# A two-layer hybrid encoder on one core: split value slabs two halves ahead, and gate and modulation slabs in half steps

## The chip, the core and the metric

The kernel runs on one core of one Trainium2 chip. The metric is the device time of one execution in microseconds (us); three runs of the kernel before gave 2033.23, 2034.02 and 2035.17 us, so the median is 2034.02 us. The engines spoken of are PE (TensorE, matrix multiply), DVE (VectorE), ACT (ScalarE) and SP (SyncE, which here issues nearly all DMAs). POOL (GpSimd) does no work of note.

## What is computed

One sequence of 256 tokens, width 1024, goes through two layers. Layer 0 mixes tokens with a gated linear recurrence (HGRN2), layer 1 with an RG-LRU block; each is followed by a PEER feed-forward part, and every sub-layer has an RMSNorm with shift, scale and gate that come from a conditioning vector (`mod = silu(c) @ w_ada + b_ada`, a 1024 x 6144 matrix for each layer). The change touches the PEER part alone:

```
def peer_ffn(h, w_q, sub_keys, u_tab, v_tab):      # 16384 experts, 8 heads, 16 experts each
    ...                                            # ids, gate: top-16 experts per token and head
    u = u_tab[idx]
    act = gelu(einsum('thkd,td->thk', u, hx))
    return einsum('thk,thkd->td', gate * act, v_tab[idx])
```

The kernel does not gather experts. It multiplies all tokens with all of `u_tab` (stage u), applies gelu, multiplies the result by a dense table of gates that is zero for experts not chosen, and multiplies that with all of `v_tab` (stage v). All weights are read from HBM once, in slabs of 128 x 2048 float32 (1 MB).

## The kernel before, in words

**Stages.** For each layer: mixer, then `peer(i)`: queries and routing, stage u (64 slabs of `u_tab`, `s1`), stage v (64 slabs of `v_tab`, `s2`). The change acts in stage v, which runs from about 711 to 1073 us in layer 0 and from 1665 to 2019 us in layer 1 of the profiled execution.

**Stage v.** A slab g holds values of 256 experts and is worked off in two halves of 128 experts. A float32 operand is split into a high and a low part of type float32r (`split`, lines 297 to 302: ACT copies the high part, DVE subtracts it to get the low part). For each half, `prep` (line 1280) splits the slab's half into a buffer of `WS` (tile `wsplit`, a ring of 3) and the gated activations of these experts into a slot of `box_wt` (tile `gsplit`, a ring of 4; lines 1288 and 1289); `mm` (line 1291) is 12 matmuls of 512 columns on line 1297: four with both high parts, four with the low part of the activations (they wait for line 1289), four with the low part of the slab. `push` (line 285) calls `prep` at once and puts `mm` into a list; as soon as the list holds more than `depth` (1) entries the oldest is emitted. So in the program the preparation of a half stands one half ahead of its matmuls. On the chip the engines run freely, and how far ACT and DVE get ahead of PE is set by the rings.

**Slabs and slots.** One list, `order`, says in which order slabs of all kinds are fetched, and `pump` (line 197) issues the next of them on SP's queue as soon as a slot of the list `allowed` is free. `take` picks the next slab of the list up, `free` returns its slot and calls `pump`. At the start of stage v only three slots (14, 15 and 16) are in `allowed`, since all others hold activations; slots 0 to 2 join after slab 17 (`release(0, 1, 2)` at line 1333, whose activations have been used), and in layer 0 five more after slab 33. A slot is free when the DVE subtraction of the slab's second half has ended.

**Other slabs in stage v.** Sixteen slabs "gd" for each layer hold the dense gates. Two of them cover the activations of eight slabs of values, so a pair stands in the list ahead of slab max(0, 8q - `GLEAD`), with `GLEAD` = 2: ahead of 0, 6, 14, 22 and so on. `gates()` (line 1238) multiplies the activations by one of them in one DVE instruction of 2048 elements per partition (line 1244); both of a pair run one after the other. In layer 0, 24 slabs "ada" (weights of the modulation) stand behind slabs 13, 15, 17 and so on; `ada_slab` (line 388) takes one in two DVE instructions of 1024 elements (line 394), one after the other. At slab 4 the residual (`XT`, 1 MB, line 1331) is read back through the same SP queue.

**Side work.** `side` emits pieces of other work after a group of matmuls: in layer 0 at the start of stage v, `load_cond` (eight small DVE, line 374, and PE, line 375, pairs and an ACT copy, line 382) and `softplus` (small DVE instructions and one ACT table load); in layer 1 after slab 44, `pre_final` (16 transposes on PE, line 1373, with ACT copies, and eight of the pairs of lines 374 and 375).

Of the kernel before, what the change touches and what calls it, by code (L numbers as in the profile page):

```python
# [16 lines left out]
AF = mybir.ActivationFunctionType  # L17
OP = mybir.AluOpType
AX = mybir.AxisListType

P = 128
# [19 lines left out]
ADA_OPEN = 4  # L41
ADA_T0 = 13
ADA_TE = 2
GLEAD = 2
GS16 = 32768.0
C_ROUTE = 1.9
C_G0 = 2.15
# [25 lines left out]
def body(ctx, tc, A, out):  # L73
# [34 lines left out]
    def slabs(v, n):  # L108
        a = at(v)
        assert a + n <= (NSL if v < NSL else NSL + NRAW)  # L110
        return AR[:, a:a + n]

    def slab(v):
        return AR[:, at(v)]
# [100 lines left out]
    def take(kind):  # L215
        n = st["taken"]
        assert order[n][0] == kind, (order[n], kind)
        assert n < st["issued"], (n, order[n])
        st["taken"] += 1
        return n, AR[:, at(held[n])]  # L220

    def free(n):
        del held[n]
        pump()
# [6 lines left out]
    def release(*slabs):  # L231
        for z in slabs:
            assert z not in allowed
            allowed.append(z)
        pump()
# [56 lines left out]
    def flush():  # L292
        while queue:
            run_one()
        run_posts(0)

    def split(raw):
        n = wsn[0] % NWS
        wsn[0] += 1
        ACT.activation(WS[:, n, 0], raw, AF.Copy)  # L300
        V.tensor_tensor(WS[:, n, 1], raw, WS[:, n, 0], op=OP.subtract)  # L301
        return WS[:, n, 0], WS[:, n, 1]

    def mm3(o, ws, rs, ks, start=True, stop=True):
        wh, wl = ws
# [79 lines left out]
        yield from row_bcast(cs, bank)  # L385
        cond_copy(bank)

    def ada_slab():
        n, raw = take("ada")
        i, s = order[n][1:]  # L390
        for m in range(2):
            col = 2 * s + m
            r_ = raw[:, m * 1024:(m + 1) * 1024]
            V.scalar_tensor_tensor(r_, r_, 1.0, cb, op0=OP.mult, op1=OP.mult, accum_out=mod[:, i, col:col + 1])  # L394
        free(n)
        if s % 4 == 3:
            c0 = 2 * (s - 3)
            V.tensor_tensor(mod[:, i, c0:c0 + 8], mod[:, i, c0:c0 + 8],
                            sv("b_ada")[:, i * 48 + c0:i * 48 + c0 + 8], op=OP.add)
            if c0 == 40:  # L400

                V.tensor_scalar(mod[:, i, c0:c0 + 8], mod[:, i, c0:c0 + 8], 1.0 / GS16, None, op0=OP.mult)

    def weaved():
        while st["taken"] < len(order) and order[st["taken"]][0] == "ada":
            ada_slab()

    epst = pool.tile([P, 2], F32, name="eps")
    V.memset(epst, EPS)
# [604 lines left out]
    def peer(i):  # L1014
# [149 lines left out]
        def aslab(j):  # L1164
            s = j // 8
            return s if s < NSL else s + 3
# [71 lines left out]
        def gates():  # L1238

            n, raw = take("gd")  # L1240
            q, th = order[n][2] // 2, order[n][2] % 2
            av = slabs(aslab(16 * q), 2).rearrange("p a (j t) -> p (a j) t", t=S)[:, :, th * P:(th + 1) * P].rearrange(
                "p j (g t) -> p j g t", t=8)
            V.tensor_tensor(av, av, raw.rearrange("p (g j t) -> p j g t", g=16, t=8), op=OP.mult)  # L1244
            free(n)

        box_wt = []
        wtn = [0]
# [1 line left out]
        def s2(cost):  # L1250
            n, raw = take("v")
            g = order[n][2]
            if g == 63 and i == 1:
                boxes = []

                def prep():
                    for half in range(2):
                        hi, lo = split(raw[:, half * 1024:(half + 1) * 1024])
                        w_ = box_wt[0][:, (wtn[0] + half) % 4]
                        ACT.activation(w_[:, 0], acol(126 + half), AF.Copy)  # L1260
                        V.tensor_tensor(w_[:, 1], acol(126 + half), w_[:, 0], op=OP.subtract)
                        boxes.append((w_, (hi, lo)))
                    free(n)

                def mm():
                    for tb in range(2):
                        for dh in range(2):
                            for z, (w_, r_) in enumerate(boxes):
                                for a, v_ in ((0, 0), (1, 0), (0, 1)):
                                    PE.matmul(PS[:, 4 + 2 * tb + dh], w_[:, a, tb * P:(tb + 1) * P],  # L1270
                                              r_[v_][:, dh * 512:(dh + 1) * 512], start=False,
                                              stop=(z, a, v_) == (1, 0, 1), skip_group_check=True)

                push(prep, mm, None, cost)
                return
            for half in range(2):
                j = 2 * g + half
                box = {}

                def prep(half=half, j=j, box=box):  # L1280
                    hi, lo = split(raw[:, half * 1024:(half + 1) * 1024])
                    if half == 1:
                        free(n)
                    z = wtn[0] % 4
                    wtn[0] += 1
                    box["v"] = (hi, lo)
                    box["z"] = z
                    ACT.activation(box_wt[0][:, z, 0], acol(j), AF.Copy)  # L1288
                    V.tensor_tensor(box_wt[0][:, z, 1], acol(j), box_wt[0][:, z, 0], op=OP.subtract)  # L1289

                def mm(j=j, box=box):
                    hi, lo = box["v"]
                    z = box["z"]
                    sets = ((0, hi), (1, hi), (0, lo))
                    steps = [(a, r, tb, dh) for a, r in sets for tb in range(2) for dh in range(2)]
                    for a, r, tb, dh in steps:
                                PE.matmul(PS[:, 4 + 2 * tb + dh], box_wt[0][:, z, a, tb * P:(tb + 1) * P],  # L1297
                                          r[:, dh * 512:(dh + 1) * 512], start=(j == 0 and a == 0 and r is hi),
                                          stop=False, skip_group_check=True)

                push(prep, mm, None, cost)
# [16 lines left out]
        if i == 0:  # L1318
            sides.append(cond)
            sides.append(softplus())  # L1320
        for it in vs[i]:
            if it[0] == "ada":
                settle(cond)
                weaved()
                continue
            if it[0] == "gd":
                gates()
                continue
            g = it[2]
            if g == 4:  # L1330
                nc.sync.dma_start(XT, Xd[i])
            elif g == 18:
                release(0, 1, 2)
            elif g == 34 and i == 0:
                release(3, 4, 5, 6, 7)
            elif g == 52 and i == 0:
                reserve(0, 1, 2, 3, 4, 5, 6)
            elif g == 58 and i == 0:
                release(13)
            s2(C_G1)  # L1340
            if g == 63 and i == 1:
                flush()
            if i == 1 and g == 44:
                sides.append(pre_final())
        if i == 0:
            release(17, 18)

# [154 lines left out]
```

## Time and profile before

| | us |
|---|---|
| median of three runs | 2034.02 |
| profiled execution, time | 2034.58 |
| profiled execution, span of the core | 2032.8 |
| stage v of layer 0, first to last matmul of line 1297 | 710.66 to 1073.05 |
| stage v of layer 1, the same | 1665.46 to 2018.81 |
| busy in the span: PE / DVE / ACT | 1952.5 / 1588.4 / 1002.4 |

PE is busy for 96% of the span, so a microsecond is won or lost where PE waits. A matmul's recorded duration overlaps its neighbours' (389 ns recorded at a distance of about 227 ns), so waits are read from start times and counts rather than from durations.

### The profile page before, as it was taken

What the parts mean: (1) busy time and instruction counts of PE and PEld (TensorE: products, weight loads), DVE (VectorE), ACT (ScalarE), POOL (GpSimd) and SP (SyncE); (2) the same over time, 40 slices, a digit from 0 to 9 for tenths busy, and PEclk for the clock granted to TensorE, in tenths of its full rate; (3) what the DMA queues carried; (4) which work ended last, traced back from release to release, by engine and by line L of the source; (5) the groups of instructions that cost most, each with busy time, mean ns of one, the idle gap of its engine ahead of it and who ended that gap; (6) DMA issues with size and microseconds to landing.
All of it is one profiled execution on the core that took longest, in us unless ns stands there. A gap on an engine that the chain in (4) does not pass through costs nothing. (4 is left out here: it accounts for less than half of the span.)

```text
span 2032.8 us, 32119 instructions
## 1 busy us (share of the span) xinstructions
PE 1952.5 (96%) x12862; PEld 1783.3 (88%) x12862; DVE 1588.4 (78%) x2791; ACT 1002.4 (49%) x1419; POOL 0.2 (0%) x4
## 2 busy tenths in 40 slices
PE   7999999999999999999999989999999999999998
PEld 6898899999999977888888889999999998888786
DVE  6798659997898777888877776998889966676575
ACT  3544544444555454444445744444545554544454
POOL 0000000000000000000000000000000000000000
PEclk9999999999999999999999999999999999999999
DMA  8654713446666767989753472444666777766561
GB/s 351 270 193 165 285 69 133 172 173 207 226 210 222 256 248 259 400 342 406 290 207 149 162 302 92 164 169 177 207 224 207 235 260 261 295 248 260 206 232 58
DMA packets 125765, 456.87 MB, mean 225 GB/s; under 512 B 7720, under 2 KB 73512, under 8 KB 74672
## 3 DMA queue, kind: packets, MB, share of 16 engines
q1 hardware_dynamic: 59056, 421.27, 55.7%
q10 hardware_dynamic: 66560, 33.56, 5.6%
q8 instruction: 100, 1.64, 0.3%
q14 instruction: 49, 0.40, 0.1%
HBM read 418.10 MB, written 36.70 MB: 224 GB/s over the span
## 5 line engine op out<-in xcount | busy, mean ns | idle before, releaser
L301 DVE TENSOR_TENSOR wsplit<-arena,wsplit 128x1024 fp32r<-128x1024 f32 x600 | 729.1, 1220 | 328.6 <-ACT wsplit L300 327.3
L300 ACT ACTIVATE wsplit<-arena 128x1024 fp32r<-128x1024 f32 x600 | 630.8, 1057 | 543.1 <-PE psum L1297 307.0
L1297 PE MATMUL psum<-wsplit,gsplit 128*128 128x512 f32 x3048 | 700.2, 391 | 8.8 <-DVE gsplit L1289 5.0
L1297 PEld LDWEIGHTS psum<-wsplit,gsplit 128*128 128x128 f32 x3048 | 572.5, 188 | 133.8 <-DVE gsplit L1289 11.0
L308 PE MATMUL psum<-hsplit,wsplit 128*128 128x256 f32 x2448 | 610.3, 287 | 1.0 <-ACT wsplit L300 0.8
L309 PE MATMUL psum<-hsplit,wsplit 128*128 128x256 f32 x2448 | 601.5, 283 | 0.0
L308 PEld LDWEIGHTS psum<-hsplit,wsplit 128*128 128x128 f32 x2448 | 470.2, 192 | 3.7 <-ACT wsplit L300 1.9
L309 PEld LDWEIGHTS psum<-hsplit,wsplit 128*128 128x128 f32 x2448 | 471.0, 192 | 0.1
L311 PE MATMUL psum<-hsplit,wsplit 128*128 128x256 f32 x2448 | 347.7, 285 | 16.8 <-DVE wsplit L301 16.7
L311 PEld LDWEIGHTS psum<-hsplit,wsplit 128*128 128x128 f32 x2448 | 316.2, 192 | 23.3 <-DVE wsplit L301 22.9
L1182 ACT ACTIVATE arena<-psum 128x512 f32<-128x512 f32 x128 | 76.1, 594 | 247.7 <-PE psum L311 247.7
L1289 DVE TENSOR_TENSOR gsplit<-arena,gsplit 128x256 fp32r<-128x256 f32 x254 | 106.1, 418 | 0.0
L1215 DVE TENSOR_TENSOR xT<-psum,xT 128x512 f32<-128x512 f32 x128 | 84.4, 684 | 22.6 <-ACT xT L1214 22.0
L1288 ACT ACTIVATE gsplit<-arena 128x256 fp32r<-128x256 f32 x254 | 101.5, 399 | 0.0
L394 DVE SCALAR_TENSOR_TENSOR arena<-arena,scratch 128x1024 f32<-128x1024 f32 x80 | 94.1, 1220 | 0.0
L1198 DVE TENSOR_TENSOR gsplit<-scratch 128x2048 f16<-128x2048 f16 x64 | 77.9, 1217 | 0.0
L1207 PE MATMUL psum<-gsplit,scratch 128*128 128x256 f16 x512 | 70.4, 274 | 5.6 <-DVE xT L1215 3.9
L1214 ACT ACTIVATE xT<-psum 128x512 f32<-128x512 f32 x128 | 71.9, 594 | 5.3 <-PE psum L1207 4.6
L1244 DVE TENSOR_TENSOR arena<-arena 128x2048 f32<-128x2048 f32 x32 | 71.9, 2284 | 0.1
L1207 PEld LDWEIGHTS <-scratch 128*128 128x128 f16 x512 | 43.8, 98 | 14.0 <-issue 6.6
L697 DVE TENSOR_TENSOR arena<-arena 128x512 f32<-128x512 f32 x56 | 35.8, 686 | 13.8 <-PE psum L688 8.6
L1196 DVE TENSOR_TENSOR scratch<-iota,T 128x1024 f16<-128x1024 f16 x64 | 43.8, 684 | 0.0
(216 smaller groups left out, 1277.8 us busy)
## 6 DMA issues: line engine op xcount, KB each, us to landing
arena<-peer_u_dram SPq DMA_DIRECT2D x128, 1024.0 KB, 4.9
arena<-peer_v_dram SPq DMA_DIRECT2D x128, 1024.0 KB, 4.9
arena<-w_ada_dram SPq DMA_DIRECT2D x40, 1024.0 KB, 5.3
gates<-xT ACTq DMA_DIRECT2D x64, 512.0 KB, 4.7
arena<-gates SPq DMA_DIRECT2D x32, 1024.0 KB, 5.0
arena<-w_q_dram SPq DMA_DIRECT2D x16, 1024.0 KB, 7.6
arena<-hg_k_dram SPq DMA_DIRECT2D x8, 1024.0 KB, 14.1
arena<-hg_s_dram SPq DMA_DIRECT2D x8, 1024.0 KB, 5.4
```

Of the source, the lines that this page charges most:

```text
L300: ACT.activation(WS[:, n, 0], raw, AF.Copy)
L301: V.tensor_tensor(WS[:, n, 1], raw, WS[:, n, 0], op=OP.subtract)
L308: PE.matmul(o, wh(k), rh(k), start=start and k == 0, stop=False)
L309: PE.matmul(o, wh(k), rl(k), start=False, stop=False)
L311: PE.matmul(o, wl(k), rh(k), start=False, stop=stop and k == ks - 1)
L394: V.scalar_tensor_tensor(r_, r_, 1.0, cb, op0=OP.mult, op1=OP.mult, accum_out=mod[:, i, col:col + 1])
L1198: V.tensor_tensor(P2[:, bf].rearrange("p t g (j z) -> p t g j z", z=2), pairs(EQ)[:, :, None].to_broadcast([P, NTB, 2, P // 2, 2]), TG[:, ...
L1207: PE.matmul(PS[:, b + t // 2, t % 2 * S:(t % 2 + 1) * S], P1[:, n % 2, 4 * h + t], P2[:, n % 2, 4 * h + t], start=True, stop=True)
L1215: V.tensor_tensor(st_, pv[:, 1], st_, op=OP.add)
L1288: ACT.activation(box_wt[0][:, z, 0], acol(j), AF.Copy)
L1289: V.tensor_tensor(box_wt[0][:, z, 1], acol(j), box_wt[0][:, z, 0], op=OP.subtract)
L1297: PE.matmul(PS[:, 4 + 2 * tb + dh], box_wt[0][:, z, a, tb * P:(tb + 1) * P], r[:, dh * 512:(dh + 1) * 512], start=(j == 0 and a == 0 and r ...
```

## The change

`depth` is 2 during stage v (1 again from slab 63 on), so that two halves are prepared in the program ahead of their matmuls. The ring of split buffers has five places: the three of `WS` and two more in the tile `H` (`hsplit`), which stage u has finished reading. The ring `box_wt` keeps its 4 slots. `GLEAD` is 3: gate pairs stand ahead of slabs 0, 5, 13, 21 and so on. A gate slab is applied in two steps of 1024 elements, and an "ada" slab in its two instructions; each `prep` of a half takes at most one such step, between the subtraction of the slab's half and the preparation of the activations (gate steps first). A pair of gates therefore occupies its two slots over the preparation of two slabs, where it used to be done in one go. What is left of gate steps is done ahead of the slab that needs them.

```diff
-GLEAD = 2
+GLEAD = 3
...
+    homes = [[WS[:, n] for n in range(NWS)]]
+
+    def widen(more):
+        n = wsn[0]
+        homes.append([homes[0][(n + z) % NWS] for z in range(NWS)] + more)
+        kept.append(n)
+        wsn[0] = 0
...
     def split(raw):
-        n = wsn[0] % NWS
+        hs = homes[-1]
+        w_ = hs[wsn[0] % len(hs)]
         wsn[0] += 1
-        ACT.activation(WS[:, n, 0], raw, AF.Copy)
-        V.tensor_tensor(WS[:, n, 1], raw, WS[:, n, 0], op=OP.subtract)
-        return WS[:, n, 0], WS[:, n, 1]
+        ACT.activation(w_[:, 0], raw, AF.Copy)
+        V.tensor_tensor(w_[:, 1], raw, w_[:, 0], op=OP.subtract)
+        return w_[:, 0], w_[:, 1]
...
-    def ada_slab():
+    def ada_parts():
+
         n, raw = take("ada")
+        return [lambda m=m: ada_part(n, raw, m) for m in range(2)]
...
+    steps_ada, steps_gate = [], []
+
+    def between():
+        for xs in (steps_gate, steps_ada):
+            if xs:
+                xs.pop(0)()
+                return
...
-            av = slabs(aslab(16 * q), 2).rearrange("p a (j t) -> p (a j) t", t=S)[:, :, th * P:(th + 1) * P].rearrange(
-                "p j (g t) -> p j g t", t=8)
-            V.tensor_tensor(av, av, raw.rearrange("p (g j t) -> p j g t", g=16, t=8), op=OP.mult)
-            free(n)
+
+            def part(z):
+                av = slab(aslab(16 * q + 8 * z)).rearrange("p (j t) -> p j t", t=S)[:, :, th * P:(th + 1) * P].rearrange(
+                    "p j (g t) -> p j g t", t=8)
+                V.tensor_tensor(av, av, raw.rearrange("p (g j t) -> p j g t", g=16, t=8)[:, 8 * z:8 * z + 8], op=OP.mult)
+                if z == 1:
+                    free(n)
+
+            steps_gate.extend([lambda: part(0), lambda: part(1)])
...
             g = order[n][2]
+            while g % 8 == 0 and steps_gate:
+                steps_gate.pop(0)()
...
                     if half == 1:
                         free(n)
+                    between()
...
+        depth[0] = 2
+        widen([H[:, n].rearrange("p k t -> p (k t)").rearrange("p (a x) -> p a x", a=2) for n in range(2)])
         for it in vs[i]:
             if it[0] == "ada":
                 settle(cond)
-                weaved()
+                steps_ada.extend(ada_parts())
                 continue
...
+            if g == 63:
+                depth[0] = 1
             s2(C_G1)
```

SP's queue at the start of stage v of layer 0, before (`gates` are gate slabs, `peer_v` slabs of values, `w_ada` modulation slabs, `resid` the residual):

```order
L212 DMA arena<-gates 128x2048 x2
L212 DMA arena<-peer_v_dram 128x2048 x6
L212 DMA arena<-gates 128x2048
L1331 DMA xT<-resid 128x2048
L212 DMA arena<-gates 128x2048
L212 DMA arena<-peer_v_dram 128x2048 x8
L212 DMA arena<-w_ada_dram 128x2048
L212 DMA arena<-gates 128x2048 x2
L212 DMA arena<-peer_v_dram 128x2048 x2
```

The same place of SP's queue after:

```order
L212 DMA arena<-gates 128x2048 x2
L212 DMA arena<-peer_v_dram 128x2048 x5
L212 DMA arena<-gates 128x2048 x2
L1372 DMA xT<-resid 128x2048
L212 DMA arena<-peer_v_dram 128x2048 x8
L212 DMA arena<-gates 128x2048 x2
L212 DMA arena<-peer_v_dram 128x2048
L212 DMA arena<-w_ada_dram 128x2048
```

The second gate pair and the residual now stand ahead of slab 5, and the third pair ahead of slab 13. With three slots in rotation that decides whose slot a slab of values gets. Before, slab 5 goes into the slot of slab 2, slab 6 into that of slab 5 and slab 7 into that of a gate slab. After, slab 5 goes into the slot of slab 4, slab 6 into that of slab 5, slab 8 into that of slab 6. At the third pair, before: slab 14 goes into the slot of the first modulation slab, slab 15 into that of a gate slab, 16 into that of 14. After: slab 13 into that of 12, 14 into that of the first gate slab, 15 into that of 14, 16 into that of 15, and 17 and 18 into those of the first two modulation slabs.

DVE's queue around the third gate pair in layer 0, before (L301 is the subtraction of a half, L1289 that of its activations, L1244 a gate slab, L394 a modulation slab):

```order
L301 TENSOR_TENSOR wsplit<-arena,wsplit 128x1024
L1289 TENSOR_TENSOR gsplit<-arena,gsplit 128x256
L394 SCALAR_TENSOR_TENSOR arena,mod<-arena,scratch 128x1024 x2
L1244 TENSOR_TENSOR arena<-arena 128x16x128 x2
L301 TENSOR_TENSOR wsplit<-arena,wsplit 128x1024
L1289 TENSOR_TENSOR gsplit<-arena,gsplit 128x256
```

The same place after (L317 is the subtraction of a half, L1328 that of its activations, L1277 half a gate slab, L413 half a modulation slab; `hsplit` is one of the two added buffers):

```order
L317 TENSOR_TENSOR wsplit<-arena,wsplit 128x1024
L1277 TENSOR_TENSOR arena<-arena 128x8x128
L1328 TENSOR_TENSOR gsplit<-arena,gsplit 128x256
L317 TENSOR_TENSOR hsplit<-arena,hsplit 128x1024
L1277 TENSOR_TENSOR arena<-arena 128x8x128
L1328 TENSOR_TENSOR gsplit<-arena,gsplit 128x256
L317 TENSOR_TENSOR hsplit<-arena,hsplit 128x1024
L1277 TENSOR_TENSOR arena<-arena 128x8x128
L1328 TENSOR_TENSOR gsplit<-arena,gsplit 128x256
L317 TENSOR_TENSOR wsplit<-arena,wsplit 128x1024
L413 SCALAR_TENSOR_TENSOR arena,mod<-arena,scratch 128x1024
L1328 TENSOR_TENSOR gsplit<-arena,gsplit 128x256
```

The four instructions on gate and modulation slabs that stood together between two halves are now six (the first gate step stands just above these rows, the second modulation step just below), each one between the subtraction of a half and that of its activations.

## Rows read from the trace of the kernel before

**Rows 1.** Page, part 1: busy us (share of the span) xinstructions.

```profile
PE 1952.5 (96%) x12862; PEld 1783.3 (88%) x12862; DVE 1588.4 (78%) x2791; ACT 1002.4 (49%) x1419; POOL 0.2 (0%) x4
```

**Rows 2.** Windows, L1297: stretch, length, PE and PEld busy, clock, DMA share.

```profile
710.60:1073.50 362.90, 353.85 (x1536) 288.17 (x1536) 1.00 0.79 307
1665.40:2019.10 353.70, 346.20 (x1512) 284.25 (x1512) 1.00 0.62 230
```

**Rows 3.** Timeline of ACT, calm stretch: start, us, instruction, [idle before, releaser].

```profile
1894.01 1.06 ACT L300 ACTIVATE wsplit<-arena 128x1024 fp32r<-128x1024 f32 x1 [1.35 <-PE psum L1297]
...
1896.73 1.06 ACT L300 ACTIVATE wsplit<-arena 128x1024 fp32r<-128x1024 f32 x1 [1.35 <-PE psum L1297]
```

**Rows 4.** Windows, line L1297, around four places where its matmuls wait.

```profile
712.00:732.00 20.00, 18.15 (x76) 13.44 (x75) 1.00 0.44 158
745.00:755.00 10.00, 9.91 (x43) 7.61 (x42) 1.00 0.89 334
790.00:800.00 10.00, 7.72 (x26) 5.55 (x26) 0.83 0.95 357
...
1905.00:1935.00 30.00, 22.66 (x90) 17.13 (x89) 0.94 0.55 197
```

**Rows 5.** Timeline of PE at the fourth gate pair of layer 0.

```profile
835.82 3.79 PE L1297 MATMUL psum<-wsplit,gsplit 128*128 128x512 f32 x16
840.55 5.73 PE L1297 MATMUL psum<-wsplit,gsplit 128*128 128x512 f32 x24 [0.94 <-DVE gsplit L1289]
```

**Rows 6.** Timeline of DVE at the same place.

```profile
834.53 4.49 DVE L1244 TENSOR_TENSOR arena<-arena 128x2048 f32<-128x2048 f32 x2
838.94 1.22 DVE L301 TENSOR_TENSOR wsplit<-arena,wsplit 128x1024 fp32r<-128x1024 f32 x1
840.07 0.42 DVE L1289 TENSOR_TENSOR gsplit<-arena,gsplit 128x256 fp32r<-128x256 f32 x1
```

**Rows 7.** DMA view, 700 to 830 us: issues, KB each, median us to landing.

```profile
arena<-peer_v_dram SPq DMA_DIRECT2D x24, 1024.0 KB, 4.9
...
xT<-resid SPq DMA_DIRECT2D x1, 1024.0 KB, 8.1
```

**Rows 8.** Timeline of SP: slab 6 of layer 1 is issued.

```profile
1691.60 0.33 SPq L212 DMA_DIRECT2D arena<-peer_v_dram  x1
```

**Rows 9.** Timeline of ACT: the same slab is split.

```profile
1696.58 1.06 ACT L300 ACTIVATE wsplit<-arena 128x1024 fp32r<-128x1024 f32 x1 [5.96 <-DMA arena<-peer_v_dram]
1697.54 0.40 ACT L1288 ACTIVATE gsplit<-arena 128x256 fp32r<-128x256 f32 x1
```

**Rows 10.** Timeline of DVE: the same slab is split.

```profile
1697.67 1.22 DVE L301 TENSOR_TENSOR wsplit<-arena,wsplit 128x1024 fp32r<-128x1024 f32 x1 [1.36 <-ACT wsplit L300]
1698.82 0.42 DVE L1289 TENSOR_TENSOR gsplit<-arena,gsplit 128x256 fp32r<-128x256 f32 x1
1699.15 1.22 DVE L301 TENSOR_TENSOR wsplit<-arena,wsplit 128x1024 fp32r<-128x1024 f32 x1
```

**Rows 11.** Timeline of ACT: slab 14 of layer 0 is waited for.

```profile
791.77 1.06 ACT L300 ACTIVATE wsplit<-arena 128x1024 fp32r<-128x1024 f32 x1 [8.53 <-DMA arena<-peer_v_dram]
```

**Rows 12.** Timeline of PE, start of stage v in layer 0.

```profile
710.66 2.99 PE L1297 MATMUL psum<-wsplit,gsplit 128*128 128x512 f32 x12
```

**Rows 13.** Timeline of DVE, start of stage v: slab 1 and slab 4.

```profile
717.76 1.22 DVE L301 TENSOR_TENSOR wsplit<-arena,wsplit 128x1024 fp32r<-128x1024 f32 x1 [5.54 <-ACT wsplit L300]
...
733.46 1.22 DVE L301 TENSOR_TENSOR wsplit<-arena,wsplit 128x1024 fp32r<-128x1024 f32 x1
```

**Rows 14.** Timeline of ACT, start of stage v.

```profile
714.13 1.03 ACT L382 ACTIVATE scratch<-psum 128x1024 f32<-128x1024 f32 x1 [5.48 <-PE psum L375]
```

**Rows 15.** Windows, all instructions, 900 to 950 us.

```profile
900.00:950.00 50.00, 49.06 (x217) 40.28 (x216) 43.01 (x60) 24.61 (x36) 0.00 (x0) 1.00 1.00 410
```

**Rows 16.** Timeline of DVE in layer 1, gates during the side work.

```profile
1916.52 4.49 DVE L1244 TENSOR_TENSOR arena<-arena 128x2048 f32<-128x2048 f32 x2
```

**Rows 17.** Timeline of PE in the same stretch.

```profile
1922.73 0.71 PE L375 MATMUL psum<-scratch,ones 128*128 128x128 f32 x4 [2.37 <-DVE scratch L374]
```

More of the change, by code (lines that the diff above doesn't have):

```diff
@@ L295, in flush, with narrow @@
         run_posts(0)
+    homes = [[WS[:, n] for n in range(NWS)]]
[4 more added lines that the diff above has]
+        wsn[0] = 0
+    kept = []
+    def narrow():
+        homes.pop()
+        wsn[0] = kept.pop()
     def split(raw):
-        n = wsn[0] % NWS
+        hs = homes[-1]
+        w_ = hs[wsn[0] % len(hs)]
         wsn[0] += 1
-        ACT.activation(WS[:, n, 0], raw, AF.Copy)
-        V.tensor_tensor(WS[:, n, 1], raw, WS[:, n, 0], op=OP.subtract)
-        return WS[:, n, 0], WS[:, n, 1]
+        ACT.activation(w_[:, 0], raw, AF.Copy)
+        V.tensor_tensor(w_[:, 1], raw, w_[:, 0], op=OP.subtract)
+        return w_[:, 0], w_[:, 1]
     def mm3(o, ws, rs, ks, start=True, stop=True):
@@ L386, in load_cond, with ada_part @@
         cond_copy(bank)
-    def ada_slab():
+    def ada_parts():
         n, raw = take("ada")
+        return [lambda m=m: ada_part(n, raw, m) for m in range(2)]
+    def ada_part(n, raw, m):
         i, s = order[n][1:]
[L391 to L394, printed above, removed]
+        col = 2 * s + m
+        r_ = raw[:, m * 1024:(m + 1) * 1024]
+        V.scalar_tensor_tensor(r_, r_, 1.0, cb, op0=OP.mult, op1=OP.mult, accum_out=mod[:, i, col:col + 1])
+        if m == 0:
+            return
         free(n)
@@ L405, in weaved @@
         while st["taken"] < len(order) and order[st["taken"]][0] == "ada":
-            ada_slab()
+            for f in ada_parts():
+                f()
+    steps_ada, steps_gate = [], []
[3 more added lines that the diff above has]
+                xs.pop(0)()
+                return
     epst = pool.tile([P, 2], F32, name="eps")
@@ L1344, in peer @@
                 sides.append(pre_final())
+        narrow()
+        while steps_ada:
+            steps_ada.pop(0)()
         if i == 0:
```

## The prediction

> **What bounds the kernel now.** I read the page's busy times first: PE works for 96% of the span [rows 1], so time can only come from or go to its waits, and DVE at 78% and ACT at 49% matter where they make PE wait. Then the two stages that the change touches [rows 2]. In a calm stretch ACT starts a half every 2.72 us and each time waits for PE [rows 3]: PE sets the pace, 2.72 us a half, 5.44 a slab, 0.227 a matmul. 128 halves are 348.2 us; layer 0's stage takes 362.9, so it waits about 14.5 us in all. Layer 1's 126 halves are 342.7 of 353.7, so some 10.5 us are waits there.
>
> Where they are, by counts: 76 matmuls (17.2 us) in 20 us at the start, 2.8 lost; 0.3 lost at 745 to 755; 26 (5.9 us) in 10 us at 790, 4.1 lost; in layer 1, 90 (20.4 us) in 30 us around the side work, 9.6 lost [rows 4]. At a gate pair 16 matmuls worth 3.6 us take 4.7, and the wait is for DVE's line 1289 [rows 5]: two gate instructions of 4.49 us together, right behind a modulation slab, keep DVE from the next half [rows 6]. Five such places in layer 0 cost 1.1 each, 5.5. That is 12.7 of the 14.5; the rest are small waits beside them.
>
> **The cycle of a slab.** This is what the forecast rests on. A slab of values lands 4.9 us after its issue in the median; the residual, among other traffic, took 8.1 [rows 7]. One slab followed through: issue at 1691.60 [rows 8]; ACT begins on it, which I call A, at 1696.58, 5.0 later [rows 9]; DVE's subtraction of the activations ends at A+2.66, that of the second half at A+3.8, and then the slot is free [rows 10]. Followed slot by slot, that is 8.8 us from issue to issue, against 5.44 that PE needs. So three slots in rotation are ample, but a chain in which each slab waits for its predecessor's slot is too slow. The wait of 8.53 us at slab 14 [rows 11] is the one place where before such a lack is long; all later splits stand behind it on ACT, and PE uses up what is prepared.
>
> **The change, part by part.**
>
> *Half steps.* 32 gate instructions become 64 of about 1.14 us (half of 2.28), and modulation instructions are spread. By the starts in [rows 10] a half takes DVE 1.48 us, with a step 2.6, under 2.72, so DVE keeps up, and all of the 5.5 us at gate pairs goes. Extra fixed cost, 32 times some 0.05 us, lies in DVE's idle time: nothing.
>
> The Trainium skill (Perfetto Trace Analysis, Optimizing Scalar/DVE Operations) advises just this: where vector engines are not saturated but cause bubbles elsewhere, break instructions up. The trace agrees on the bubble of 1.1 us [rows 5]; by the rule alone the outcome would be the first rival below.
>
> *Five buffers, four activation slots.* The activations of half n still wait for the matmuls of half n-4, and the split of the next half stands behind them on ACT. So a slab's second half is split 0.40 + 1.06 + 1.22 = 2.7 us after the matmuls of the first half two slabs earlier end. PE is due to start the *next* slab, at a time I call T, five halves after that end, so the slot is free at T-10.9. With three buffers a half waits for the one three earlier, and the slot is free 4 to 5 us later. The buffers in `H` cost nothing: stage u is done with them, and the next norm comes after stage v.
>
> *Where steps go into the cycle.* A step sits between DVE's two instructions of a half, so in a slab that carries steps the activations are ready at A+3.8 instead of 2.66, the second half is split at A+4.95, and the first half's matmuls end at A+5.6 (eight of 0.227 still to do). If the next slab has to use this slot, its A is 4.95 + 5.0 = 9.95 later: 9.95 - 5.44 = 4.5 us lost for each such link.
>
> *Start of layer 0.* PE begins at 710.66 [rows 12] behind pairs with DVE that now follow two prepared halves instead of one: one half's DVE work, 1.47, later, 712.1. The second half of slab 1 no longer has slab 0's wait, so the 2.8 goes but for 0.4. DVE's unbroken run of splits and softplus from 717.76 on ends slab 4 at 734.7 [rows 13]; after, it starts about 1 us later (ACT's copy at 714.13 [rows 14] moves with PE) and has one half less to do. I keep 734.7.
>
> *Slabs 5 and 6, layer 0.* Slab 5 now stands behind both gates and the residual and takes slab 4's slot: issue 734.7, with the residual's 8.1 in front A = 742.9 (with 5.0 it would be 739.7). PE is due at 712.1 + 10 x 2.72 + 0.4 = 739.7. The first half ends at 748.5 instead of 742.4: 6.1 lost (2.9 without the residual). Slab 6 takes slab 5's slot: 4.5 more. Slab 7 has a gate slab's slot, and slab 8 is in time. Sum 10.6.
>
> *Slabs 13 to 18, layer 0.* Slab 13 takes 12's slot, 10.9 before T, so A = T-5.9, its last gate step ends at T+0.2, and only then slab 14 gets its slot, with a modulation slab 1.1 us ahead of it in the queue: landing T+5.1 alone, T+6.5 if they share the 410 GB/s of [rows 15] (2.5 us a slab). With A = T+6.6 the half ends at T+12.2; due is T+8.2: 4.0 lost. Slab 15 in 14's slot: 4.5. Slab 16 in 15's: 4.5. Slab 17 is in time, 18 (in a modulation slab's slot, freed a step later) loses 1.5. Then slots 0 to 2 join. Sum 14.5; with A at 4.9 flat and no sharing 12.
>
> *Clock.* Around the wait at 790 the granted clock is 0.83 over 10 us, a mix of its two levels (2.4 and 1.2 GHz) behind PE's standstill [rows 4]: 1.7 us of work lost. The five long waits bring the like, but part of it falls where the matmuls wait for line 1289 anyway: 0 to 1.7 each, I take 0.5, together 2.5.
>
> The Trainium skill (TensorE: Matmul & The Clock Gate, HAM oscillation — how this bites in real kernels) says that waits for DMA between groups of matmuls throw the clock to half each time. The rows at 790 agree; by it all five would cost 1.7, 8.5 in place of 2.5, and the sum would be 6 higher.
>
> *Layer 1.* No softplus and no modulation slabs. Slab 5: A = T-5.4, in time; slab 6 in its slot: A6 = T+4.55, ends T+10.15 against T+8.2, 2.0 lost. Slab 14 here takes 13's own slot, issue T-0.95, half ends T+9.65: 1.5 lost. Later pairs have six slots. In the side work a gate pair of 4.49 [rows 16] holds up the small DVE instruction that PE waits 2.37 for [rows 17]; in half steps this goes: -2.4, with the clock -3. Waits of PE on its own transposes stay. Small waits at 6 and 14 that go: -0.6. Net about 0, bounds -4 to +4.
>
> **Sum.** Layer 0: -14.5 (all waits of before) + 1.4 + 0.4 + 10.6 + 14.5 + 2.5 = +15. Layer 1: 0. The profiled execution took 2034.58 (span 2032.8), 0.56 above the median: 2049.6 there, 2049 as a median. Bounds from the small ends (slab 5 at 2.9, 12, clock 0, layer 1 -4): +3; from the large ones: +25.
>
> **Rivals.**
>
> *The lead carries every slab (faster).* Slots free 4 to 5 us earlier; if that is enough, all waits of layer 0 go but the start: -14.5 + 1.8, and -3.6 in layer 1: 2018. It decides if slabs 6 and 15 were issued before their predecessors are split, that is with one more slot. For it: [rows 5, 6]. Against: the list gives them those very slots.
>
> *A wash.* If the landings are at the short end and DVE runs further ahead at the start, links of some 2 us in place of 4.5 bring 14 us, what layer 0 gives back: 2034. For it: a slab often lands in 4.9. Against: link and step are fixed by [rows 9, 10].
>
> *It goes on past slab 18.* DMA engines are fully busy at 900 to 950 us [rows 15]; PE, late with few slabs in hand, meets this burst, two or three more links and all clock losses come: +26, 2060. Against: a later PE also asks for less.
>
> **How the numbers follow.** Forecast 0.72 (own range 2040 to 2056), past slab 18 0.12, wash 0.07, faster 0.09. A difference under 0.2%, 4 us, can't be told from none: faster 0.10, same 0.06, slower 0.84. The range is 2035 to 2060: it leaves out the faster rival and a little of the long one.
>
> **What would show it.** Right: ACT's waits for slabs of values grow from one of 8.5 to several in 740 to 835, PE's gaps there come in pairs (one for ACT's high parts, then four matmuls, then one for the subtraction of the activations), the waits at gate pairs past 839 are gone, and layer 0's stage is about 15 us longer while layer 1's is alike. Wrong: no DMA waits near 742 or 800 to 825; waits of 1.1 us that stay would say that DVE is behind; a stage in layer 1 that changes by more than 4 either way that I mis-sized the lead.

## The result, and the profile after

The changed kernel takes 2046.16 us in the median of four runs (2045.79 to 2049.37), the kernel before 2034.16 in four (2033.23 to 2035.17): 1.0058 times as long, with a 95% interval of 1.0046 to 1.0070. The change makes the kernel slower by 12.0 us. The profiled execution took 2046.52 us, 11.94 more than that of before.

Time by engine of the profile after (busy us, share of the span, instructions); of the 11.9 us by which the span has grown, 2.8 are busy time of PE and the rest is idle:

```profile
span 2044.7 us, 32152 instructions
PE 1955.3 (96%) x12862; PEld 1785.4 (87%) x12862; DVE 1598.6 (78%) x2823; ACT 1000.9 (49%) x1419; POOL 0.2 (0%) x4
```

Stretches of stage v in the profile after, the matmul line (now L1336) alone; columns as in [rows 2], which these answer to, as well as [rows 4]:

```profile
712.60:1087.30 374.70, 359.84 (x1536) 292.82 (x1536) 0.97 0.77 299
712.00:732.00 20.00, 19.08 (x83) 15.45 (x84) 1.00 0.40 149
740.00:757.00 17.00, 10.86 (x33) 7.34 (x32) 0.80 0.41 153
800.00:832.00 32.00, 24.02 (x75) 17.38 (x76) 0.79 0.51 193
836.00:844.00 8.00, 8.00 (x37) 6.64 (x36) 1.00 1.01 425
1678.40:2031.00 352.60, 344.58 (x1512) 283.33 (x1512) 1.00 0.61 231
1919.00:1949.00 30.00, 24.19 (x103) 18.80 (x103) 1.00 0.58 218
```

At 0.227 us each, the 33 matmuls of 740 to 757 are 7.5 us of work in 17, the 75 of 800 to 832 are 17.0 in 32. At the gate pair past 836 PE is now busy throughout, and at the start nearly so. From first to last matmul, layer 0's stage is longer by 11.8 us (374.2 against 362.4) and starts 2.1 later; layer 1's stage is 1.1 shorter.

The waits of ACT for slabs of values in the profile after (total us, times, the longest; the second buffer name is that of the added split buffers), and ahead of them those of before:

```profile
ACT wsplit L300 <- DMA arena<-peer_v_dram: 38.4, 9, 8.5
```

```profile
ACT wsplit L316 <- DMA arena<-peer_v_dram: 95.7, 25, 12.9
ACT hsplit L316 <- DMA arena<-peer_v_dram: 29.9, 12, 10.6
```

The longest wait was 8.5 before [rows 11] and is 12.9 now. I call a row of slabs that each come late behind the one before a chain, and each step of it a link. The first chain follows in order of time. PE in the profile after (start, duration, engine, line, operation, count, and in brackets the idle time before it and what ended it):

```profile
735.10 5.60 PE L1336 MATMUL psum<-hsplit,gsplit 128*128 128x512 f32 x24
744.52 2.08 PE L1336 MATMUL psum<-wsplit,gsplit 128*128 128x512 f32 x4 [3.82 <-ACT gsplit L1327]
746.94 6.58 PE L1336 MATMUL psum<-wsplit,gsplit 128*128 128x512 f32 x20 [0.35 <-DVE gsplit L1328]
754.27 1.20 PE L1336 MATMUL psum<-wsplit,gsplit 128*128 128x512 f32 x4 [0.75 <-ACT gsplit L1327]
756.69 2.12 PE L1336 MATMUL psum<-wsplit,gsplit 128*128 128x512 f32 x8 [1.22 <-DVE gsplit L1328]
758.65 1.53 PE L1336 MATMUL psum<-hsplit,gsplit 128*128 128x512 f32 x6
```

SP's queue after, from the second gate pair on; a row covers several issues, its time is that of the first. The last row is one of the eight issues of the row above it, that of slab 6:

```profile
727.23 5.43 SPq L212 DMA_DIRECT2D arena<-gates  x2
732.71 0.42 SPq L1372 DMA_DIRECT2D xT<-resid  x1
735.27 34.41 SPq L212 DMA_DIRECT2D arena<-peer_v_dram  x8
```

```profile
748.05 0.33 SPq L212 DMA_DIRECT2D arena<-peer_v_dram  x1
```

ACT and then DVE in the same chain:

```profile
743.10 1.06 ACT L316 ACTIVATE wsplit<-arena 128x1024 fp32r<-128x1024 f32 x1 [12.85 <-DMA arena<-peer_v_dram]
752.85 1.06 ACT L316 ACTIVATE wsplit<-arena 128x1024 fp32r<-128x1024 f32 x1 [7.13 <-DMA arena<-peer_v_dram]
```

```profile
744.19 1.23 DVE L317 TENSOR_TENSOR wsplit<-arena,wsplit 128x1024 fp32r<-128x1024 f32 x1 [8.61 <-ACT wsplit L316]
745.34 1.22 DVE L1277 TENSOR_TENSOR arena<-arena 128x1024 f32<-128x1024 f32 x1
746.47 0.42 DVE L1328 TENSOR_TENSOR gsplit<-arena,gsplit 128x256 fp32r<-128x256 f32 x1
746.81 1.22 DVE L317 TENSOR_TENSOR wsplit<-arena,wsplit 128x1024 fp32r<-128x1024 f32 x1
747.94 1.22 DVE L1277 TENSOR_TENSOR arena<-arena 128x1024 f32<-128x1024 f32 x1
```

Slab 5 is issued at 735.27, behind the residual, and ACT begins on it at 743.10. DVE splits its first half, does half a gate slab, and only then the activations: the four matmuls with both high parts wait 3.82, the next eight wait again for line 1328. The second half is split by 748.0, slab 5's slot is free, slab 6 is issued at 748.05, and ACT begins on it at 752.85: 9.75 after slab 5, where PE needs one every 5.44.

The second chain, on PE in the profile after:

```profile
802.60 2.07 PE L1336 MATMUL psum<-hsplit,gsplit 128*128 128x512 f32 x4 [2.97 <-ACT gsplit L1327]
805.02 6.59 PE L1336 MATMUL psum<-hsplit,gsplit 128*128 128x512 f32 x20 [0.35 <-DVE gsplit L1328]
812.40 1.20 PE L1336 MATMUL psum<-wsplit,gsplit 128*128 128x512 f32 x4 [0.79 <-ACT gsplit L1327]
814.84 4.87 PE L1336 MATMUL psum<-wsplit,gsplit 128*128 128x512 f32 x20 [1.24 <-DVE gsplit L1328]
822.15 1.88 PE L1336 MATMUL psum<-wsplit,gsplit 128*128 128x512 f32 x4 [2.44 <-ACT gsplit L1327]
824.59 3.78 PE L1336 MATMUL psum<-wsplit,gsplit 128*128 128x512 f32 x8 [0.56 <-DVE gsplit L1328]
828.17 6.14 PE L1336 MATMUL psum<-hsplit,gsplit 128*128 128x512 f32 x24
```

Slabs 14, 15 and 16 begin at 802.60, 812.40 and 822.15: 9.80 and 9.75 apart.

I use one measure for all kernels below: how much longer than 5.44 us it takes from one slab's first matmul to the next one's. Before, layer 0 loses 3.1 in slabs 0 and 1, 4.7 in slabs 6, 13 and 14, and 1.2 to 1.3 at each of five gate pairs (6.2 together); layer 1 loses 9.8 in slabs 44 to 46. After, layer 0 loses 0.6 in slab 0, 10.0 in slabs 4 to 6 and 15.6 in slabs 13 to 16, so the two chains are 25.6 of the 26.2 that it loses; layer 1 loses 2.7 in slabs 6 and 14 and 6.8 in 44 and 45.

### The profile page after: what moved, and what is told of

It is laid out like the page before. It is cut to its first block, busy times and chain, and to the rows that moved or that the text cites. A ratio compares the mean times of both kernels' runs of the same rounds, so it can differ in the third digit from the quotient of the medians.

```text
span 2044.7 us, 32152 instructions
## 1 busy us (share of the span) xinstructions
PE 1955.3 (96%) x12862; PEld 1785.4 (87%) x12862; DVE 1598.6 (78%) x2823; ACT 1000.9 (49%) x1419; POOL 0.2 (0%) x4
## 5 line engine op out<-in xcount | busy, mean ns | idle before, releaser
L317 DVE TENSOR_TENSOR wsplit<-arena,wsplit 128x1024 fp32r<-128x1024 f32 x500 | 606.5, 1219 | 232.7 <-ACT wsplit L316 231.8
L316 ACT ACTIVATE wsplit<-arena 128x1024 fp32r<-128x1024 f32 x500 | 522.7, 1052 | 298.4 <-DMA arena<-peer_v_dram 95.7
L1336 PE MATMUL psum<-wsplit,gsplit 128*128 128x512 f32 x1848 | 435.8, 393 | 12.3 <-ACT gsplit L1327 7.8
L1336 PEld LDWEIGHTS psum<-wsplit,gsplit 128*128 128x128 f32 x1848 | 348.9, 190 | 89.0 <-ACT gsplit L1327 9.5
L1336 PE MATMUL psum<-hsplit,gsplit 128*128 128x512 f32 x1200 | 284.3, 393 | 4.3 <-ACT gsplit L1327 3.0
L1336 PEld LDWEIGHTS psum<-hsplit,gsplit 128*128 128x128 f32 x1200 | 227.3, 190 | 53.3 <-ACT gsplit L1327 3.4
L317 DVE TENSOR_TENSOR hsplit<-arena,hsplit 128x1024 fp32r<-128x1024 f32 x100 | 122.2, 1222 | 43.1 <-ACT hsplit L316 42.6
L1328 DVE TENSOR_TENSOR gsplit<-arena,gsplit 128x256 fp32r<-128x256 f32 x254 | 106.8, 420 | 49.5 <-ACT gsplit L1327 49.4
L316 ACT ACTIVATE hsplit<-arena 128x1024 fp32r<-128x1024 f32 x100 | 104.7, 1047 | 30.1 <-DMA arena<-peer_v_dram 29.9
L413 DVE SCALAR_TENSOR_TENSOR arena<-arena,scratch 128x1024 f32<-128x1024 f32 x80 | 95.8, 1218 | 0.0
L1277 DVE TENSOR_TENSOR arena<-arena 128x1024 f32<-128x1024 f32 x64 | 77.5, 1218 | 0.0
## 6 DMA issues: line engine op xcount, KB each, us to landing
arena<-hg_k_dram SPq DMA_DIRECT2D x8, 1024.0 KB, 15.6
```

The lines of the kernel that those rows point to most:

```text
L316: ACT.activation(w_[:, 0], raw, AF.Copy)
L317: V.tensor_tensor(w_[:, 1], raw, w_[:, 0], op=OP.subtract)
```

## The experiments

My theory: half steps (gates and modulation) hold two of three slots over the preparation of two slabs, so slab 14 waits for a gate slab's slot, and slabs 6, 15 and 16 each wait for their predecessor's. (Slab 5 waits for slab 4's slot by its place in the list, whether steps are halved or not.) Rivals: the place of the pairs in the list (`GLEAD`) does it; the deeper lead with its buffers does it; the half step's place ahead of the activations does it. Every kernel was timed in five rounds (`pair_apart` and `before_h_slots` have eleven runs) beside the kernel before, whose median was 2034.2 to 2034.9 each time. Ratios are to the kernel before, with the 95% interval.

**One part undone or alone.** `whole_steps`: the changed kernel, with steps done at once.

```diff
-            steps_gate.extend([lambda: part(0), lambda: part(1)])
+            for z in range(2):
+                part(z)
...
-                steps_ada.extend(ada_parts())
+                for f in ada_parts():
+                    f()
```

> The changed kernel, but a gate pair and a modulation slab are taken in one go again, as before; position of the gates (ahead of slab 5, 13, ...), depth 2 and five split buffers stay. Slot theory (the loss comes from two of three slots being held by half-used gate slabs, so that slabs 6, 14, 15, 16 of layer 0 wait for the slot of their predecessor): the slots come back at once, the waits near 745 and 802 to 829 go, the five 1.1 us waits at gate pairs stay gone because four prepared halves cover 4.5 us of DVE: 2024 to 2030 us. Rival A (the earlier place of the gates alone makes the slabs late): about 2046 as now. Rival B (depth 2 and the buffers in H are what costs): 2040 or more.

Measured: 2022.92 us (0.9947, 0.9933 to 0.9960), 23 less than with half steps. The chain at slabs 13 to 16 is gone; against my expectation slab 5 still comes late. PE in its trace there, and ACT's waits:

```profile
743.70 11.04 PE L1337 MATMUL psum<-wsplit,gsplit 128*128 128x512 f32 x36 [4.32 <-ACT gsplit L1328]
754.57 5.60 PE L1337 MATMUL psum<-hsplit,gsplit 128*128 128x512 f32 x24
```

```profile
ACT wsplit L316 <- DMA arena<-peer_v_dram: 37.3, 13, 13.4
```

One wait of 4.32 for the slab behind the residual, and no second link: slab 6 follows at once. ACT waits 37.3 us for slabs in these buffers, where it was 95.7. What is lost behind the wait is the clock, 11.04 for 36 matmuls that take 8.32 elsewhere in this trace. So slabs 4 to 6 lose 7.2 even with whole steps: by this comparison half steps cost only 2.8 of the 10.0 of the first chain, while the 15.6 of the second are theirs. The other 7.2 belong to the place of the gates and the residual ahead of slab 5; with `GLEAD` 2 (`buffers_only` below) 1.7 is lost there.

`glead3_only`: the kernel before with the pairs one slab earlier.

```diff
-GLEAD = 2
+GLEAD = 3
```

> The kernel before with one edit: gate pairs stand ahead of slabs 0, 5, 13, ... instead of 0, 6, 14, .... Slot theory: slots come back at once, so no chain forms; slab 5 is late by about as much as in the changed kernel without its links (0 to 3 us in layer 0), and the gates no longer stand directly behind a modulation slab on DVE, so the five waits of 1.1 us shrink: 2027 to 2035 us. Rival A (place alone): 2042 or more.

Measured: 2024.74 us (0.9954, 0.9941 to 0.9968). The place of the pairs alone gains 9.5, more than I expected: all five waits at gate pairs go, and the side work of layer 1 loses 5.8 instead of 9.8; slabs 4 and 5 of layer 0 lose 3.5. DVE before, just ahead of [rows 6]:

```profile
832.24 1.22 DVE L394 SCALAR_TENSOR_TENSOR arena<-arena,scratch 128x1024 f32<-128x1024 f32 x1
833.39 1.22 DVE L394 SCALAR_TENSOR_TENSOR arena<-arena,scratch 128x1024 f32<-128x1024 f32 x1
```

DVE in the trace of `glead3_only` at the fourth pair (some rows between are left out):

```profile
822.31 1.22 DVE L394 SCALAR_TENSOR_TENSOR arena<-arena,scratch 128x1024 f32<-128x1024 f32 x1
...
823.88 1.22 DVE L301 TENSOR_TENSOR wsplit<-arena,wsplit 128x1024 fp32r<-128x1024 f32 x1
...
825.36 1.22 DVE L301 TENSOR_TENSOR wsplit<-arena,wsplit 128x1024 fp32r<-128x1024 f32 x1
...
826.83 4.49 DVE L1244 TENSOR_TENSOR arena<-arena 128x2048 f32<-128x2048 f32 x2
831.23 1.22 DVE L301 TENSOR_TENSOR wsplit<-arena,wsplit 128x1024 fp32r<-128x1024 f32 x1
```

The pair no longer stands right behind a modulation slab: a slab of values lies between them. The wait of before was for 2.4 us of modulation and 4.49 of gates in a row, not for the gates alone. Layer 1 of the kernel before agrees: it has the same gate pairs and no modulation slabs, and at the four pairs ahead of slabs 22, 30, 38 and 54 it loses nothing that shows (under 0.1).

`buffers_only`: the changed kernel with whole steps and `GLEAD` 2, so that the deeper lead and the five buffers are left alone.

```diff
-GLEAD = 3
+GLEAD = 2
...
-            steps_gate.extend([lambda: part(0), lambda: part(1)])
+            for z in range(2):
+                part(z)
...
-                steps_ada.extend(ada_parts())
+                for f in ada_parts():
+                    f()
```

> Depth 2 and five split buffers alone: gates ahead of slabs 0, 6, 14, ... and taken whole, modulation slabs whole, as before. Slot theory: slots come back 4 to 5 us earlier than before, nothing holds them: the waits at gate pairs in layer 0 (5.5 us) go, the wait at slab 14 (4.1 us) shrinks: 2024 to 2030 us. Rival B (depth 2 or H costs time): 2034 or more.

Measured: 2022.79 us (0.9939, 0.9925 to 0.9952), a little less than expected. Two halves ahead also cover the gate pairs, without moving them. Neither place nor lead makes the kernel slower; each alone gains 9.5 to 11.8. Together they gain no more (`whole_steps`, 11.3): both remove the waits at gate pairs, and what the place gives in the side work of layer 1 (5.7 lost there instead of 9.7) it takes at slab 5. Of those 9.7 a wait behind a whole gate pair is one part, as in the kernel before [rows 16, 17]; PE in layer 1 of `buffers_only`:

```profile
1909.90 2.09 PE L391 MATMUL psum<-scratch,ones 128*128 128x128 f32 x8 [2.51 <-DVE scratch L390]
```

Half steps with `GLEAD` 2 were not run: by the list, a modulation slab and two gate slabs ahead of slab 14 of layer 0 would hold all three slots, and their steps stand in the preparation of slab 14.

`no_h_buffers`: the changed kernel with the ring of three split buffers.

```diff
-        widen([H[:, n].rearrange("p k t -> p (k t)").rearrange("p (a x) -> p a x", a=2) for n in range(2)])
...
-        narrow()
```

> The changed kernel without the two split buffers in H (ring of three again); half steps, place of gates and depth 2 stay. Slot theory: a slot comes back 4 to 5 us later in the calm cycle, which adds that much to the first wait of each chain that is not already late for another reason (slab 14 of layer 0, slabs 6 and 14 of layer 1), and steps can again hold PE up at later gate pairs: 2056 to 2064 us. Rival B (the buffers in H cost time): below 2046. If the number of buffers is indifferent: 2046.

Measured: 2066.57 us (1.0161, 1.0147 to 1.0174), more than expected. Slots come free later, and the chains grow: 10.4 in slabs 4 to 6 and 19.5 in 13 to 16 of layer 0, and in layer 1 links of 4.1 and 4.4 (slabs 5, 6), 4.4 and 3.3 (slabs 13, 14), where the changed kernel has none of full size. So the buffers do bring slots back earlier, as the prediction's cycle says; under half steps they gain 20 us, most of it (15.8) in layer 1, and it is not enough.

**More slots.** `h_as_slots`: the changed kernel, with the memory of `H` as two more slots for whole slabs instead of two split buffers, from slab 1 on.

```diff
...
-        widen([H[:, n].rearrange("p k t -> p (k t)").rearrange("p (a x) -> p a x", a=2) for n in range(2)])
...
+            elif g == 1:
+                HR.append(pool.tile([P, 2, SL], F32, name="hsplit", tag="hsplit"))
+                release(19, 20)
...
-        narrow()
...
```

> The changed kernel, but the 16 KB of H serve as two more raw slots from slab 1 on (slots 19 and 20, given back after slab 52 in layer 0) and not as split buffers (ring of three). Half steps, place of gates and depth 2 stay. Slot theory: with five slots no slab waits for its predecessor's slot, all chains go, and the waits at gate pairs are gone as well: 2019 to 2026 us, clearly under before. Rival C (the half step between DVE's two instructions of a half is what PE waits for): the waits near 745 and 802 to 829 stay in some part, 2034 or more.

Measured: 2022.52 us (0.9945, 0.9931 to 0.9958). Half steps, `GLEAD` 3 and depth 2 are all in it. Its windows (the same two as above) and ACT's waits:

```profile
740.00:757.00 17.00, 17.00 (x77) 14.08 (x76) 1.00 0.91 335
800.00:832.00 32.00, 32.00 (x143) 26.50 (x142) 1.00 0.99 401
```

```profile
ACT wsplit L320 <- DMA arena<-peer_v_dram: 6.0, 3, 2.8
```

Both chains are gone, and the DMA engines carry 335 and 401 GB/s where they carried 153 and 193: PE was short of slots, not of bandwidth. This is the prediction's first rival with its condition met and more: two more slots where it asked for one, 2022.5 where it gave 2018.

`before_h_slots`: the same two slots in the kernel before.

```diff
...
+            elif g == 1:
+                HR.append(pool.tile([P, 2, SL], F32, name="hsplit", tag="hsplit"))
+                release(19, 20)
...
```

> The kernel before with H's 16 KB as two more raw slots from slab 1 on; nothing else is changed. Slot theory: only the waits for slabs go, that is 4.1 us at slab 14 of layer 0 and some tenths at slabs 6 and 14 of layer 1; the 5.5 us at gate pairs, the start and the side work stay: 2028 to 2031 us. If slots are not what slab 14 waits for: 2034.

Measured: 2030.63 us (0.9979, 0.9970 to 0.9988). Slots remove what slots caused, 3.5 of the 4.7 in slabs 6, 13 and 14; the 1.2 left at slab 14 and the five 1.2 to 1.3 behind it are those of the gate pairs.

**The half step's place, and the residual.** `step_behind`: the step comes behind the subtraction of the activations.

```diff
-                    between()
                     z = wtn[0] % 4
...
                     V.tensor_tensor(box_wt[0][:, z, 1], acol(j), box_wt[0][:, z, 0], op=OP.subtract)
+                    between()
```

> The changed kernel with the step moved behind the subtraction of the activations, so that the activations of a half are ready 1.1 us earlier; the second half is split, and the slot free, at the same time as now. Slot theory: links of 4.5 us each stay, only the last half of each chain gains 1.1 us: two chains in layer 0, two single waits in layer 1, so 2042 to 2045 us. Rival C (the step in that place is the cost): most of the loss goes, 2036 or less.

Measured: 2045.75 us (1.0052, 1.0038 to 1.0065): just above the range expected, and no gain that can be told. The losses at slabs 4 to 6 (10.4) and 13 to 18 (15.8) stay. In layer 1 the waits at slabs 6 and 14 all but go (0.3 instead of 2.7), and slab 0 of layer 0 loses 1.6 more. DVE does the same work per slab in another order, and the slot is returned as late. That the place ahead of the activations makes the chains is refuted.

`resid_late`: the residual is read at slab 26.

```diff
-            if g == 4:
+            if g == 26:
```

> The changed kernel, but the residual (1 MB) is read back at slab 26 instead of slab 4, so that it no longer stands in the queue ahead of slab 5. Slot theory: slab 5 lands 5 us after its issue instead of 8; its wait in layer 0 falls from about 6 to about 3 us: 2042 to 2044 us. If the residual does not matter: 2046.

Measured: 2043.60 us (1.0048, 1.0034 to 1.0062). The runs reach from 2042.45 to 2048.17, and this interval overlaps that of the changed kernel, so the time alone doesn't show the gain. The trace shows its place:

```profile
739.22 1.19 PE L1336 MATMUL psum<-wsplit,gsplit 128*128 128x512 f32 x4 [1.44 <-ACT gsplit L1327]
741.64 8.63 PE L1336 MATMUL psum<-wsplit,gsplit 128*128 128x512 f32 x24 [1.23 <-DVE gsplit L1328]
```

Slab 5 lands 5.4 us after its issue instead of 7.8, and its wait is 1.44 instead of 3.82, and slabs 4 to 6 lose 7.6 instead of 10.0; the link to slab 6 is as long as before.

**Half steps without the held slots.** `pair_apart`: the two gate slabs of a pair stand two slabs apart in the list, so that one is done before the next takes a slot.

```diff
-                    if max(0, 8 * q - GLEAD) == it[2]:
-                        zs += [("gd", i, 2 * q), ("gd", i, 2 * q + 1)]
+                    for th in range(2):
+                        if max(0, 8 * q - 4 + 2 * th) == it[2]:
+                            zs.append(("gd", i, 2 * q + th))
```

> The changed kernel, but the two gate slabs of a pair stand apart in the list: the first ahead of slab 8q-4, the second ahead of slab 8q-2 (for the first pair, both ahead of slab 0). Half steps for gates and modulation slabs, depth 2 and five buffers stay. Slot theory, followed through the list: slab 6 now gets the slot of the first gate slab and 7 that of slab 5, so the chain at slabs 5 and 6 goes in both layers, and so does slab 14's wait; in layer 0 slab 15 still takes 14's slot and 16 takes 15's, while modulation slabs hold the others, so 1.5 + 4.5 + 1.5 us stay there: 2026 to 2033 us. Rival C (half steps themselves are the cost): 2042 or more.

Measured: 2032.28 us (0.9985, 0.9976 to 0.9994). The first chain shrinks from 10.0 to 3.2 (I expected no wait there), the second from 15.6 to 9.5, where the modulation slabs still go in half steps.

`pair_apart_ada_whole`: the same, with modulation slabs done at once.

```diff
-                steps_ada.extend(ada_parts())
+                for f in ada_parts():
+                    f()
```

> As pair_apart, and modulation slabs are taken whole again, so that their slot comes back at once. Slot theory: slab 15 gets the first modulation slab's slot and 16 a gate slab's, no chain is left anywhere though gates are still applied in half steps: 2019 to 2025 us. Rival C (half steps): 2034 or more.

Measured: 2021.67 us (0.9931, 0.9918 to 0.9945). The second chain falls to 1.0. All gates are still in half steps here, and the kernel is 13.2 us faster than before: no cost of half steps can be told where the slab's slot is not wanted (`whole_steps` took 2022.92). Slabs 5 and 6 still lose 2.9. The two edits gain 24.5 over the changed kernel, in this order 13.9 by the pair and 10.6 by the modulation slabs; in the other order the shares could differ.

**A version that beats both.** `slots_and_spread`: `h_as_slots`, and in layer 1's side work one group of transposes for each half.

```diff
-            yield 0.3
+            yield 1.45
```

> As h_as_slots (two raw slots in H, half steps, depth 2), and the side work after slab 44 of layer 1 is spread: one group of transposes behind each half in place of several behind one. If PE's 8 us of waits there come from its turns with ACT (0.2 to 0.26 us between transposes) and from ACT being held, some go: 2018 to 2022 us. If they are PE's own transposes: 2022.5 as h_as_slots.

Measured: 2019.06 us (0.9919, 0.9906 to 0.9933), the lowest median: 15.8 less than the kernel before beside it. The side work loses 5.3 in slabs 44 to 48 instead of 6.8. The interval just overlaps that of `h_as_slots`, whose median is 3.5 higher, and the trace shows 1.5 of that; the rest is not shown.

## Why the prediction was right

Direction and the mechanism of the loss held; of +15 came +12. The gains came in about the size forecast, though not shown to come for the reason given. By the prediction's steps:

- *Slabs 5 and 6.* A was put at 742.9 and the next slab's ACT at 9.95 later, 752.85; measured 743.10 and 752.85. That the second is met exactly is luck: A came 0.2 later and the step to the next slab was 0.2 shorter. The term was 10.6, measured 10.0. The residual's 8.1 in front of slab 5 was 7.8.
- *Slabs 13 to 18.* The links were put at 4.0, 4.5 and 4.5. Up to the end of slab 16's first half PE loses 15.1; without the slow matmuls of that half (1.8), 13.3, against 13.0. The 1.5 at slab 18 did not come, so this step of the sum failed. PE was by then late enough, as I read it: where it was less late, slab 18 did lose 1.2 (`resid_late`) and 1.5 (`pair_apart`).
- *Link cost.* 4.5 forecast; 9.75 to 9.80 measured from slab to slab, so 4.3 to 4.4.
- *Clock.* I took 2.5 in all; 2.3 shows, but not as I split it. The clock falls at both chains (0.80 and 0.79 above), and 20 matmuls take 6.58 and 6.59 where the same count takes 4.83 at full clock in layer 1 of this trace. Yet PE then waits again, 0.75 and 0.79, for a slab whose time the slots set, and what it lost is hidden in that wait. Only behind the last wait, at 824.59 and 828.17, is it paid: 8 matmuls in 3.78 instead of 2.0, 24 in 6.14 instead of 5.60. In the kernel that the Trainium skill describes (TensorE: Matmul & The Clock Gate, HAM oscillation — how this bites in real kernels), each wait for DMA throws the clock to half. Here matmuls slowed behind three of the five waits for slabs (3.82, 2.97 and 2.44) and not behind those of 0.75 and 0.79; a sum of 8.5 for five waits would have been 6 too high.
- *Gate pairs.* All waits there went, 6.2 against the 5.5 given. The prediction names the modulation slab in front of the pair, but credits half steps with the cure. No run shows that: with whole steps the place alone (`glead3_only`) and the lead alone (`buffers_only`) each remove them all.
- *Start.* 2.1 later instead of 1.4, and 0.6 lost instead of 0.4. The 2.1 is within the spread given at the end of this section.
- *Layer 1.* Put at 0, measured -1.1: slabs 6 and 14 lose 2.7 instead of 3.5, and the side work gains the 3.0 forecast. That 3.0 is luck. The prediction has half steps free the small DVE instruction; but `glead3_only` gains 4.0 there with whole steps, since the pair then stands ahead of slab 45 and no longer in front of that instruction, and `buffers_only` gains 0.1. Half steps add 1.1 to the loss (6.8 against 5.7 in `whole_steps`). In the prediction's first paragraph 353.7 less 342.7 is 11.0, not some 10.5; nothing is worked out from it.

So 1.1 of the 3 us are in layer 0 (slab 18 and the first chain, partly balanced by the start), 0.8 between the stages, 1.1 in layer 1. The advice of the Trainium skill (Perfetto Trace Analysis, Optimizing Scalar/DVE Operations) to break instructions up where they cause bubbles on other engines would by itself have forecast a faster kernel. Here the bubbles went, but they go with whole instructions too, and the advice leaves out what the pieces hold: `whole_steps` is 23 us faster than the broken-up version.

Not settled: why the start of stage v differs by 1 to 3 us between kernels whose code ahead of it is alike; I compared stages from their own starts for that reason.

## What to carry to other kernels

Before work is spread out, ask what it holds while it is spread: a piece that keeps a prefetch slot twice as long can cost more than the stall it removes. Follow one slot through its cycle (issue, landing, last reader); where each load takes its predecessor's slot, the loss per load is that cycle less the pace of the bound engine, here 9.8 - 5.4. Edits that remove the same waits gain once, so try each alone before they are combined.

## What the runs showed of the hardware

How little standstill costs the clock surprised me. Behind one wait of 3.82 us, and also behind two of 1.44 and 1.23 with four matmuls between (`resid_late`), matmuls ran at half rate for a while: behind the pair, 24 took 8.63 us instead of 5.60. Behind waits of 0.79 and 1.24 in the second chain, 20 took 4.87, full rate. One wait by itself does not tell, either: behind the 2.44 of the second chain the clock fell (granted clock 0.50 from 822.4 to 829.2), behind the single wait of 2.79 at slab 5 of `glead3_only` it stayed at its upper level (granted clock 1.00). The window there, then PE:

```profile
744.00:754.00 10.00, 8.93 (x38) 7.04 (x39) 1.00 0.80 302
```

```profile
744.98 21.35 PE L1297 MATMUL psum<-wsplit,gsplit 128*128 128x512 f32 x91 [2.79 <-ACT gsplit L1288]
```

The price was 1.8 to 3.0 us each time. It was paid in full where no further wait for data followed (2.7 in `whole_steps`, 2.3 behind the second chain), and hidden, in whole or in part, where PE had to wait for the next slab anyway.
